# Joining the two matmuls that share their weights in the MLP block products

## The chip, the cores and the metric

The kernel runs on one core of one Trainium2 chip, in one launch. The metric is the device time of one execution in microseconds (us). Three timed runs of the kernel before gave 2880.28, 2886.01 and 2888.11 us; the median is 2886.01 us. One further execution was profiled; it took 2884.02 us.

The engines are called by their names here: TensorE (in the profile PE for its matmuls and PEld for its weight loads), VectorE (DVE), ScalarE (ACT), GpSimd (POOL) and SyncE (SP), which issues the transfers. PSUM is the memory that TensorE writes its products to, in banks of 128 partitions x 512 float32; SBUF is the memory that holds everything else on the core.

## The reference

One layer of an encoder over 512 tokens with a model width of 2048: a mixer (neighbourhood attention and a gated delta rule), then an MLP, then a last normalisation. The change touches only the MLP. In the reference it is:

```python
hn = _rmsnorm(h, norm_mlp_w)
h = h + jnp.square(jax.nn.relu(hn @ w_mlp_up)) @ w_mlp_down
return _rmsnorm(h, norm_final_w)
```

`w_mlp_up` is 2048 x 8192 and `w_mlp_down` 8192 x 2048, both float32, as is the result.

## The kernel before

**Layout.** Activations lie transposed: 128 features in the partitions, the 512 tokens along the free axis. A unit of weights is a tile of 128 partitions x 1024 columns: eight blocks of 128 x 128 for one group of 128 output features, j = 0 to 7.

**Two parts for each operand.** Float32 numbers are multiplied as two parts in the type fp32r: a high part (a cast by ScalarE, tiles `wh`) and a low part (what the cast left over, subtracted by VectorE, tiles `wl`). `split`, lines 93 to 96, makes both. A product takes three matmuls: high x high, high x low and low x high.

**Block products.** The MLP multiplies in 2 x 2 blocks by a scheme with seven block products where the plain way has eight. The weights of a *pair* of output groups are four units: A11, A12, A21, A22. The 512 tokens are halved too. So a product is one weight unit, or a sum of units, times a moving operand of 1024 x 256. Each moving operand (names 11, 21, 22 and T1 to T4) lies ready in eight tiles of 128 x 512: columns 0 to 255 (`lo_t`) hold the high part, columns 256 to 511 (`hi_t`) the low part (`fill`, lines 857 to 859). The products are called Q4, P1, P5, P6, P3, P7 and P2, and stand in this order (`ORDER`, line 919). `run_product` (928 to 959) makes the weight sums S1 to S4 on VectorE, splits the weights, and calls `product` (899 to 908), which issues three matmuls of 256 columns for each j: lines 904, 905 and 906. Lines 904 and 905 have the same weights, the high part, and the two halves of the moving tile; all three add into the same 256 columns of one bank. Some products go on adding in a bank in which an earlier product already stands (`BANK` and `FIRST`, lines 917 and 918): P6 and P7 onto P1, P3 onto P5. So an earlier product is taken out before the next one adds to its bank.

**The up half.** 32 pairs, u0 to u31. `up_evac` (969 to 997) takes each product out of its bank: Q4, P5, P1 and P6 are copied to SBUF by ScalarE (tiles tA and tB), and P7, P3 and P2 are added to these copies by VectorE, which reads the bank. Then VectorE takes the minimum (r1) or maximum (r0) with zero and multiplies by the token's norm factor, ScalarE squares, and `differences` (1001 to 1011) makes the moving operands of the down half with four VectorE instructions and writes them to DRAM (`hidD`).

**The down half.** Four blocks b of the inner dimension, eight pairs each (names d0_0 to d3_7), two pairs at a time (`down_group`, 1079 to 1112). The first group of each block also loads and splits the moving operands (`operand_fill`, 1072 to 1077: 56 splits of 256 columns). Each product is added to or subtracted from the residual tiles h0 and h1 by VectorE, which reads the bank. `store` (1116 to 1129) writes them back to DRAM; the last group of the last block (pairs d3_6 and d3_7, with its own order of products, `keep`) stays on the core and ends the kernel with the final norm (`finish`, 1144 to 1153), in which GpSimd takes every third multiplication (line 1148).

**What sets the order.** Each engine works its own instructions in the order in which they stand. A scheduler places them: casts and low halves stand some two products ahead of the product that uses them. Tile pools hold the buffers: three for `wh` and `wl`, four for the raw weight units, seven for the tiles `a` of A22, A21 and of sums (line 1033), six for `et`, seven PSUM banks (line 785). A tile is written again only when its last reader is done. SyncE issues the transfers, one after the other.

Of the kernel before, what the change touches and what calls it, by code (L numbers as in the profile page):

```python
# [49 lines left out]
def tile_hybrid_block(  # L50
# [733 lines left out]
    with ExitStack() as p1:  # L784
# [76 lines left out]
        with ExitStack() as p5:  # L861
# [37 lines left out]
            def product(ps, w, o, first=False):  # L899
                hi, lo = w  # L900
                for j in range(8):
                    t = XS[o, j]
                    c = slice(j * 128, (j + 1) * 128)
                    PE.matmul(ps, hi[:, c], t[:, lo_t], start=first and j == 0, stop=False, skip_group_check=True)  # L904
                    PE.matmul(ps, hi[:, c], t[:, hi_t], start=False, stop=False, skip_group_check=True)  # L905
                    PE.matmul(ps, lo[:, c], t[:, lo_t], start=False, stop=j == 7, skip_group_check=True)  # L906
                    if j % NPUMP == NPUMP - 1:
                        pump()
# [12 lines left out]
            def open_pair(nm, a11, a12):  # L921
                p = Pair()
                p.nm, p.ps, p.step = nm, {}, 0
                p.a11, p.a12 = a11, a12
                p.keep = False
                return p

            def run_product(p, q, sums):
# [27 lines left out]
                if bk not in p.ps:  # L956
                    p.ps[bk] = bank()[:, 0:256]
                product(p.ps[bk], w, ROLE[q], q in FIRST)
# [10 lines left out]
            def up_evac(i, p, q, et):  # L969
# [5 lines left out]
                tA, tB, r0, r1 = p.tA, p.tB, p.r0, p.r1  # L975
                if q == "Q4":
                    S_.copy(out=tA[:, 0], in_=ps)
                elif q == "P5":
                    S_.copy(out=tA[:, 1], in_=ps)
                elif q == "P1":  # L980
                    S_.copy(out=tB[:, 0], in_=ps)
                elif q == "P6":
                    S_.copy(out=tB[:, 1], in_=ps)  # L983
                elif q == "P7":
                    add(r1.rearrange("p (o t) -> p o t", o=2), ps[:, None, :].to_broadcast([128, 2, 256]), tA)
                    V.scalar_tensor_tensor(out=r1, in0=r1, scalar=0.0, in1=rB, op0=ALU.min, op1=ALU.mult)
                    S_.activation(out=r1, in_=r1, func=AF.Square)
                elif q == "P3":
                    add(r0[:, hi_t], ps, tB[:, 1])
                else:  # L990
                    add(r0[:, lo_t], ps, tB[:, 0])
# [29 lines left out]
            for i, p in enumerate(first):  # L1021
                for q in ("P1", "P2"):
                    w = heads[i, q] or wsplit(p.a12, f"{q}_u{i}")
                    p.ps[BANK[q]] = bank()[:, 0:256]
                    product(p.ps[BANK[q]], w, ROLE[q], True)
# [3 lines left out]
        with ExitStack() as p6:  # L1029
            sm = p6.enter_context(tc.tile_pool(name="sm", bufs=1, side="right", reuse_waits="tile"))  # L1030

            def a_tile(name):
                return sm.tile([128, 1024], F32, tag="a", name=name, bufs=7)

            def et(name):
                return sm.tile([128, 2, 256], F32, tag="et", name=name, bufs=6)

# [5 lines left out]
            def up_group(idx, order, ps=None):  # L1043
# [4 lines left out]
                if order[0] == "P1":  # L1048
                    for q in ("P1", "P2"):
                        for i, p in zip(idx, ps):  # L1050
                            up_evac(i, p, q, et)
                    order = order[2:]
                for n, q in enumerate(order):
                    for i, p in zip(idx, ps):
                        run_product(p, q, a_tile)
                        up_evac(i, p, q, et)
# [22 lines left out]
            def down_group(b, idx, order, done):  # L1079
                ps = []  # L1080
                for i in idx:
                    p = open_pair(f"d{b}_{i}", load_raw(wdn[2 * i, 2 * b], f"A11_d{b}_{i}"), load_raw(wdn[2 * i, 2 * b + 1], f"A12_d{b}_{i}"))
                    more(p, wdn[2 * i + 1, 2 * b + 1], wdn[2 * i + 1, 2 * b])
                    p.keep = order is not ORDER
                    ps.append(p)
# [5 lines left out]
                for q in order:  # L1091
                    if idx[0] == 0:
                        operand_fill(b, ROLE[q])
                    for i, p in zip(idx, ps):
                        t = run_product(p, q, a_tile)
                        h0, h1 = p.h0, p.h1
                        if q == "Q4":
# [187 lines left out]
```

## Time and profile before

| what | value |
|---|---|
| median of three runs | 2886.01 us (2880.28 to 2888.11) |
| profiled execution: its time, its span | 2884.02 us, 2881.9 us |
| TensorE matmul busy | 2811.9 us, 98% of the span |
| TensorE weight load busy | 2538.3 us, 88% |
| VectorE busy | 2065.1 us, 72% |
| ScalarE busy | 1167.0 us, 40% |
| GpSimd busy | 24.8 us, 1% |

The span is the time from the first to the last instruction of the profiled execution. "Busy" counts an instruction from its start to its end; matmuls overlap, so their rate is read from the distance between starts, not from their length. In the rows "L904" is line 904 of the kernel, "out<-in" names the tiles, "x768" how many instructions the row stands for.

### The profile page before, as it was taken

Reading aid. Unit: us, or ns where it says so; the run is one execution under the profiler, and the core shown is the slowest. Engines: PE = TensorE matmul, PEld = TensorE weight load, DVE = VectorE, ACT = ScalarE, POOL = GpSimd, SP = SyncE. Lnnn points to the kernel's source line nnn. Section 1 sums busy time; section 2 is a strip of 40 time slices with the busy share of each in tenths; the row PEclk is TensorE's granted clock in tenths of the full one; section 3 lists DMA queues with packets and bytes.
Section 4 is the critical chain, followed back from the end, with each engine's and each line's share of the span. In section 5 each row is a group of like instructions: output and inputs, shape, how many; then the busy total and the mean of one; then the engine's idle time right before and its main releaser. Section 6 shows DMA issues by size and latency. Waiting matters only on the chain.

```text
span 2881.9 us, 45456 instructions
## 1 busy us (share of the span) xinstructions
PE 2811.9 (98%) x17944; PEld 2538.3 (88%) x17944; DVE 2065.1 (72%) x3131; ACT 1167.0 (40%) x1869; POOL 24.8 (1%) x66
## 2 busy tenths in 40 slices
PE   8999999999999999999999999999998999999997
PEld 6778788888788888888888999999998999999997
DVE  6888769845564444444447888888888888898987
ACT  6444322223233333322335444444445354444543
POOL 0000010000000000000000000000000000000000
PEclk9999999999999999999999999999999999999998
DMA  7555663555642222533443445454447566565644
GB/s 228 191 187 189 196 198 120 183 173 182 181 140 93 87 93 84 199 133 125 142 145 137 153 151 156 143 162 147 149 146 228 180 222 201 170 226 174 221 133 146
DMA packets 217493, 469.32 MB, mean 163 GB/s; under 512 B 38976, under 2 KB 80000, under 8 KB 217280
## 3 DMA queue, kind: packets, MB, share of 16 engines
q1 hardware_dynamic: 216608, 464.33, 49.9%
q8 instruction: 140, 2.29, 0.3%
q0 software_dynamic: 672, 2.10, 0.3%
q14 instruction: 73, 0.60, 0.1%
HBM read 379.15 MB, written 87.20 MB: 162 GB/s over the span
## 4 chain that ended last, share of the span: by engine, by line
PE 78%; DMA 9%; DVE 9%; ACT 2%; issue 1%; SPq 0%; DVEq 0%; ACTq 0%
PE ps_b L906 12%; PE ps_b L904 12%; PE ps_b L905 12%; PE ps_mm L115 8%; PE ps_mm L117 8%; PE ps_mm L116 8%; PE ps_b L115 4%; PE ps_b L116 4%; PE ps_b L117 4%; DMA hr<-hidD 1%; DVE wl_S_d L95 1%; DVE wl_in L90 1%; DMA bB<-rowD 1%; DMA hTD<-h 1%; DMA Nd<-bB 1%
## 5 line engine op out<-in xcount | busy, mean ns | idle before, releaser
L115 PE MATMUL ps_mm<-xh,wh_in 128*128 128x512 f32 x1416 | 567.1, 400 | 3.1 <-ACT wh_in L89 3.1
L117 PE MATMUL ps_mm<-xh,wl_in 128*128 128x512 f32 x1416 | 559.9, 395 | 0.5 <-DVE wl_in L90 0.5
L116 PE MATMUL ps_mm<-xl,wh_in 128*128 128x512 f32 x1416 | 559.8, 395 | 0.0
L89 ACT CAST wh_in<-raw_in 128x1024 fp32r<-128x1024 f32 x177 | 186.0, 1051 | 412.9 <-PE ps_mm L116 328.5
L117 PEld LDWEIGHTS ps_mm<-xh,wl_in 128*128 128x128 f32 x1416 | 267.7, 189 | 60.4 <-DVE wl_in L90 1.0
L115 PEld LDWEIGHTS ps_mm<-xh,wh_in 128*128 128x128 f32 x1416 | 267.7, 189 | 58.6 <-ACT wh_in L89 3.5
L116 PEld LDWEIGHTS ps_mm<-xl,wh_in 128*128 128x128 f32 x1416 | 267.7, 189 | 55.0 <-issue 0.2
L90 DVE TENSOR_TENSOR wl_in<-raw_in,wh_in 128x1024 fp32r<-128x1024 f32 x177 | 216.2, 1222 | 118.7 <-ACT wh_in L89 110.2
L904 PE MATMUL ps_b<-XT_h,wh_S_d 128*128 128x256 f32 x768 | 220.8, 287 | 10.6 <-ACT wh_S_d L94 10.6
L906 PE MATMUL ps_b<-XT_h,wl_S_d 128*128 128x256 f32 x768 | 220.9, 288 | 3.2 <-DVE wl_S_d L95 3.1
L905 PE MATMUL ps_b<-XT_h,wh_S_d 128*128 128x256 f32 x768 | 219.8, 286 | 0.0
L906 PE MATMUL ps_b<-XT_x,wl_S_u 128*128 128x256 f32 x768 | 217.4, 283 | 0.8 <-DVE wl_S_u L95 0.8
L904 PE MATMUL ps_b<-XT_x,wh_S_u 128*128 128x256 f32 x768 | 217.4, 283 | 0.5 <-ACT tB_u L983 0.5
L905 PE MATMUL ps_b<-XT_x,wh_S_u 128*128 128x256 f32 x768 | 217.3, 283 | 0.0
L94 ACT CAST wh_S_u<-A_u 128x1024 fp32r<-128x1024 f32 x128 | 134.3, 1050 | 147.2 <-DVE A_u L911 81.2
L94 ACT CAST wh_S_d<-A_d 128x1024 fp32r<-128x1024 f32 x124 | 129.6, 1047 | 148.2 <-PE ps_b L905 129.0
L95 DVE TENSOR_TENSOR wl_S_u<-A_u,wh_S_u 128x1024 fp32r<-128x1024 f32 x128 | 156.0, 1222 | 39.4 <-ACT wh_S_u L94 39.4
L95 DVE TENSOR_TENSOR wl_S_d<-A_d,wh_S_d 128x1024 fp32r<-128x1024 f32 x124 | 151.2, 1222 | 23.9 <-ACT wh_S_d L94 22.2
L904 PEld LDWEIGHTS ps_b<-XT_h,wh_S_d 128*128 128x128 f32 x768 | 149.8, 195 | 12.5 <-ACT wh_S_d L94 12.5
L906 PEld LDWEIGHTS ps_b<-XT_h,wl_S_d 128*128 128x128 f32 x768 | 149.9, 195 | 5.0 <-DVE wl_S_d L95 5.0
L905 PEld LDWEIGHTS ps_b<-XT_h,wh_S_d 128*128 128x128 f32 x768 | 149.9, 195 | 0.0
L906 PEld LDWEIGHTS ps_b<-XT_x,wl_S_u 128*128 128x128 f32 x768 | 147.2, 192 | 1.0 <-DVE wl_S_u L95 1.0
(393 smaller groups left out, 7033.9 us busy)
## 6 DMA issues: line engine op xcount, KB each, us to landing
raw_in<-in_win SPq DMA_DIRECT2D x177, 512.0 KB
raw_A_u<-in_wup SPq DMA_DIRECT2D x64, 512.0 KB
A_u<-in_wup SPq DMA_DIRECT2D x64, 512.0 KB
A_d<-in_wdn SPq DMA_DIRECT2D x64, 512.0 KB
raw_A_d<-in_wdn SPq DMA_DIRECT2D x64, 512.0 KB
raw_wo<-in_wout SPq DMA_DIRECT2D x32, 512.0 KB
h<-hTD SPq DMA_DIRECT2D x64, 256.0 KB
hTD<-h SPq DMA_DIRECT2D x60, 256.0 KB
```

The costliest lines, as they stand in the source:

```text
L89: S_.copy(out=hi, in_=raw)
L90: V.tensor_tensor(out=lo, in0=raw, in1=hi.bitcast(F32), op=ALU.subtract)
L94: S_.copy(out=hi, in_=src)
L95: V.tensor_tensor(out=lo, in0=src, in1=hi.bitcast(F32), op=ALU.subtract)
L115: PE.matmul(ps, hi[:, w], rh, start=first and kk == 0, stop=False)
L116: PE.matmul(ps, hi[:, w], rl, start=False, stop=False)
L117: PE.matmul(ps, lo[:, w], rh, start=False, stop=last and kk == 7)
L904: PE.matmul(ps, hi[:, c], t[:, lo_t], start=first and j == 0, stop=False, skip_group_check=True)
L905: PE.matmul(ps, hi[:, c], t[:, hi_t], start=False, stop=False, skip_group_check=True)
L906: PE.matmul(ps, lo[:, c], t[:, lo_t], start=False, stop=j == 7, skip_group_check=True)
```

## The change

In `product` the two matmuls with the high weights become one of 512 columns: the high weights times the whole moving tile, into a whole bank of 512 columns. The low weights times the high half go, as before, into columns 0 to 255. For j = 7 the two stand the other way round. The product is then the sum of the bank's two halves. Every product's bank is copied whole by ScalarE into a tile `u` of SBUF (`spill`, pool tag "pr", two buffers), and GpSimd adds: where VectorE added from the bank before, and also the left to the right half. The seven `a` tiles become six. The last two pairs of the down half (`keep`) have the old form throughout. The weight sums, splits, ReLU steps, differences and fills stay on VectorE and ScalarE.

```diff
--- before.py
+++ after.py
@@ -896,11 +896,18 @@
                 lo = st.tile([128, 1024], F32R, tag="wl", name=f"wl_{name}", bufs=3)
                 return split(raw, hi, lo)
 
-            def product(ps, w, o, first=False):
+            def product(ps, w, o, first=False, whole=True):
                 hi, lo = w
                 for j in range(8):
                     t = XS[o, j]
                     c = slice(j * 128, (j + 1) * 128)
+                    if whole:
+                        mms = [(ps, hi, t), (ps[:, lo_t], lo, t[:, lo_t])]
+                        for n, (dst, a, b) in enumerate(mms if j < 7 else mms[::-1]):
+                            PE.matmul(dst, a[:, c], b, start=first and j + n == 0, stop=j == 7 and n == 1, skip_group_check=True)
+                        if j % NPUMP == NPUMP - 1:
+                            pump()
+                        continue
                     PE.matmul(ps, hi[:, c], t[:, lo_t], start=first and j == 0, stop=False, skip_group_check=True)
                     PE.matmul(ps, hi[:, c], t[:, hi_t], start=False, stop=False, skip_group_check=True)
                     PE.matmul(ps, lo[:, c], t[:, lo_t], start=False, stop=j == 7, skip_group_check=True)
@@ -923,6 +930,7 @@
                 p.nm, p.ps, p.step = nm, {}, 0
                 p.a11, p.a12 = a11, a12
                 p.keep = False
+                p.whole = True
                 return p
 
             def run_product(p, q, sums):
@@ -954,8 +962,8 @@
                     w = wsplit(p.s2, f"S4_{nm}")
                 bk = BANK[q]
                 if bk not in p.ps:
-                    p.ps[bk] = bank()[:, 0:256]
-                product(p.ps[bk], w, ROLE[q], q in FIRST)
+                    p.ps[bk] = bank() if p.whole else bank()[:, lo_t]
+                product(p.ps[bk], w, ROLE[q], q in FIRST, p.whole)
                 return p.ps[bk]
 
             def up_m(i):
@@ -966,29 +974,31 @@
                 m0, m1 = up_m(i)
                 return open_pair(f"u{i}", load_raw(wup[m0, 0], f"A11_u{i}"), load_raw(wup[m0, 1], f"A12_u{i}"))
 
-            def up_evac(i, p, q, et):
+            def gsum(out, x, y, op=ALU.add):
+                G.tensor_tensor(out=out, in0=x, in1=y, op=op)
+
+            def up_evac(i, p, q, et, spill):
                 ps = p.ps[BANK[q]]
                 if not hasattr(p, "tA"):
                     p.tA, p.tB = et(f"tA_u{i}"), et(f"tB_u{i}")
                     p.r0, p.r1 = ev(f"r0_u{i}"), ev(f"r1_u{i}")
                     p.left = 7
                 tA, tB, r0, r1 = p.tA, p.tB, p.r0, p.r1
+                u = spill(ps, f"u{q}_u{i}")
                 if q == "Q4":
-                    S_.copy(out=tA[:, 0], in_=ps)
+                    gsum(tA[:, 0], u[:, 0], u[:, 1])
                 elif q == "P5":
-                    S_.copy(out=tA[:, 1], in_=ps)
-                elif q == "P1":
-                    S_.copy(out=tB[:, 0], in_=ps)
-                elif q == "P6":
-                    S_.copy(out=tB[:, 1], in_=ps)
+                    gsum(tA[:, 1], u[:, 0], u[:, 1])
                 elif q == "P7":
-                    add(r1.rearrange("p (o t) -> p o t", o=2), ps[:, None, :].to_broadcast([128, 2, 256]), tA)
+                    gsum(u[:, 0], u[:, 0], u[:, 1])
+                    gsum(r1.rearrange("p (o t) -> p o t", o=2), u[:, 0:1, :].to_broadcast([128, 2, 256]), tA)
                     V.scalar_tensor_tensor(out=r1, in0=r1, scalar=0.0, in1=rB, op0=ALU.min, op1=ALU.mult)
                     S_.activation(out=r1, in_=r1, func=AF.Square)
-                elif q == "P3":
-                    add(r0[:, hi_t], ps, tB[:, 1])
                 else:
-                    add(r0[:, lo_t], ps, tB[:, 0])
+                    dst = r0[:, lo_t] if q in ("P1", "P2") else r0[:, hi_t]
+                    gsum(dst, dst if q in ("P2", "P3") else u[:, 1], u[:, 0])
+                    if q in ("P2", "P3"):
+                        gsum(dst, dst, u[:, 1])
                 p.left -= 1
                 if p.left:
                     return
@@ -1021,7 +1031,7 @@
             for i, p in enumerate(first):
                 for q in ("P1", "P2"):
                     w = heads[i, q] or wsplit(p.a12, f"{q}_u{i}")
-                    p.ps[BANK[q]] = bank()[:, 0:256]
+                    p.ps[BANK[q]] = bank()
                     product(p.ps[BANK[q]], w, ROLE[q], True)
             for o, j in early_fill[8:]:
                 fill(o, j, tr_src[o, j])
@@ -1030,10 +1040,15 @@
             sm = p6.enter_context(tc.tile_pool(name="sm", bufs=1, side="right", reuse_waits="tile"))
 
             def a_tile(name):
-                return sm.tile([128, 1024], F32, tag="a", name=name, bufs=7)
+                return sm.tile([128, 1024], F32, tag="a", name=name, bufs=6)
 
             def et(name):
                 return sm.tile([128, 2, 256], F32, tag="et", name=name, bufs=6)
+
+            def spill(ps, name):
+                u = sm.tile([128, 2, 256], F32, tag="pr", name=name, bufs=2)
+                S_.copy(out=u.rearrange("p a b -> p (a b)"), in_=ps)
+                return u
 
             def more(p, s22, s21):
                 p.a22, p.a21 = a_tile(f"A22_{p.nm}"), a_tile(f"A21_{p.nm}")
@@ -1048,12 +1063,12 @@
                 if order[0] == "P1":
                     for q in ("P1", "P2"):
                         for i, p in zip(idx, ps):
-                            up_evac(i, p, q, et)
+                            up_evac(i, p, q, et, spill)
                     order = order[2:]
                 for n, q in enumerate(order):
                     for i, p in zip(idx, ps):
                         run_product(p, q, a_tile)
-                        up_evac(i, p, q, et)
+                        up_evac(i, p, q, et, spill)
                     if n == 2:
                         while late:
                             late.pop(0)()
@@ -1082,6 +1097,7 @@
                     p = open_pair(f"d{b}_{i}", load_raw(wdn[2 * i, 2 * b], f"A11_d{b}_{i}"), load_raw(wdn[2 * i, 2 * b + 1], f"A12_d{b}_{i}"))
                     more(p, wdn[2 * i + 1, 2 * b + 1], wdn[2 * i + 1, 2 * b])
                     p.keep = order is not ORDER
+                    p.whole = not p.keep
                     ps.append(p)
                 for e in (1, 0):
                     for i, p in zip(idx, ps):
@@ -1094,7 +1110,17 @@
                     for i, p in zip(idx, ps):
                         t = run_product(p, q, a_tile)
                         h0, h1 = p.h0, p.h1
-                        if q == "Q4":
+                        if p.whole:
+                            u = spill(t, f"u{q}_{p.nm}")
+                            if q == "P7":
+                                gsum(u[:, 0], u[:, 0], u[:, 1])
+                                hv = h1.rearrange("p (o t) -> p o t", o=2)
+                                gsum(hv, hv, u[:, 0:1, :].to_broadcast([128, 2, 256]), ALU.subtract)
+                            else:
+                                dst = (h1 if q in ("Q4", "P5") else h0)[:, lo_t if q in ("Q4", "P1", "P2") else hi_t]
+                                for k in range(2):
+                                    gsum(dst, dst, u[:, k], ALU.subtract if q in ("Q4", "P5") else ALU.add)
+                        elif q == "Q4":
                             add(h1[:, lo_t], h1[:, lo_t], t, ALU.subtract)
                         elif q == "P5":
                             add(h1[:, hi_t], h1[:, hi_t], t, ALU.subtract)
```

On **ScalarE**, in up pair 10 from the copy of Q4 on, there stood (ps_b is a bank, wh_S2, wh_S4, wh_S3 are casts of the weights of P6, P3 and P7; tA and tB are the copies of banks):

```order
L977 COPY tA_u10_14553<-ps_b_14528 128x256
L996 ACTIVATE r0_u9_14320<-r0_u9_14320 128x512
L94 CAST wh_S2_u10_14629<-A22_u10_14520 128x1024
L981 COPY tB_u10_14554<-ps_b_14562 128x256
L94 CAST wh_S4_u10_14659<-A22_u10_14520 128x1024
L979 COPY tA_u10_14553<-ps_b_14593 128x256
L94 CAST wh_S3_u10_14689<-A21_u10_14521 128x1024
```

and now stand (uQ4, uP1, uP5, uP6 are the bank copies into the two "pr" tiles):

```order
L94 CAST wh_S1_u10_14187<-A22_u10_14130 128x1024
L1006 ACTIVATE r0_u9_13961<-r0_u9_13961 128x512
L1050 COPY uQ4_u10_14159<-ps_b_14138 128x512
L94 CAST wh_S2_u10_14221<-A22_u10_14130 128x1024
L1050 COPY uP1_u10_14183<-ps_b_14166 128x512
L94 CAST wh_S4_u10_14245<-A22_u10_14130 128x1024
L1050 COPY uP5_u10_14208<-ps_b_14191 128x512
L94 CAST wh_S3_u10_14270<-A21_u10_14131 128x1024
L1050 COPY uP6_u10_14241<-ps_b_14166 128x512
```

Each product now has a 512-wide copy, and it stands ahead of the cast of the weights that come three products later.

On **VectorE**, at the change from pair 9 to pair 10, there stood (r1_u9 and r0_u9 are pair 9's results, A22_u10 and A21_u10 weights or their sums, wl low parts):

```order
L95 TENSOR_TENSOR wl_A22_u10_14525<-A22_u10_14520,wh_A22_u10_14524 128x1024
L911 TENSOR_TENSOR A22_u10_14520<-A22_u10_14520,A21_u10_14521 128x1024
L911 TENSOR_TENSOR r1_u9_14321<-ps_b_14327,tA_u9_14318 128x512
L95 TENSOR_TENSOR wl_A11_u10_14559<-raw_A11_u10_14516,wh_A11_u10_14558 128x1024
L986 SCALAR_TENSOR_TENSOR r1_u9_14321<-r1_u9_14321,rB_79 128x512
L911 TENSOR_TENSOR A21_u10_14521<-A21_u10_14521,raw_A11_u10_14516 128x1024
L911 TENSOR_TENSOR r0_u9_14320<-ps_b_14293,tB_u9_14319 128x256
L95 TENSOR_TENSOR wl_S1_u10_14590<-A22_u10_14520,wh_S1_u10_14589 128x1024
```

and now stand:

```order
L95 TENSOR_TENSOR wl_A22_u10_14135<-A22_u10_14130,wh_A22_u10_14134 128x1024
L918 TENSOR_TENSOR A22_u10_14130<-A22_u10_14130,A21_u10_14131 128x1024
L918 TENSOR_TENSOR A21_u10_14131<-A21_u10_14131,raw_A11_u10_14126 128x1024
L995 SCALAR_TENSOR_TENSOR r1_u9_13962<-r1_u9_13962,rB_79 128x512
L95 TENSOR_TENSOR wl_A11_u10_14163<-raw_A11_u10_14126,wh_A11_u10_14162 128x1024
L1005 SCALAR_TENSOR_TENSOR r0_u9_13961<-r0_u9_13961,rB_79 128x512
L95 TENSOR_TENSOR wl_S1_u10_14188<-A22_u10_14130,wh_S1_u10_14187 128x1024
```

The two additions that read a bank (r1_u9 and r0_u9 from ps_b) are gone; the ReLU steps of r1_u9 and r0_u9 still stand ahead of the low parts of A11 and S1 of pair 10.

On **GpSimd**, which had nothing to do in the MLP before, now stand for pair 10 ("x2" are two such instructions in a row):

```order
L978 TENSOR_TENSOR tA_u10_14155<-uQ4_u10_14159 128x256
L978 TENSOR_TENSOR r0_u10_14157<-uP1_u10_14183 128x256
L978 TENSOR_TENSOR tA_u10_14155<-uP5_u10_14208 128x256
L978 TENSOR_TENSOR r0_u10_14157<-uP6_u10_14241 128x256
L978 TENSOR_TENSOR r0_u10_14157<-r0_u10_14157,uP3_u10_14265 128x256 x2
L978 TENSOR_TENSOR uP7_u10_14290<-uP7_u10_14290 128x256
L978 TENSOR_TENSOR r1_u10_14158<-uP7_u10_14290,tA_u10_14155 128x512
L978 TENSOR_TENSOR r0_u10_14157<-r0_u10_14157,uP2_u10_14316 128x256 x2
```

Ten instructions: nine additions of 256 columns and one of 512, and GpSimd, not VectorE, now hands r0 and r1 to the ReLU step.

## Rows read from the trace of the kernel before

**Rows 1.** The page's head and part 1: busy us, share of span, instructions.
```profile
span 2881.9 us, 45456 instructions
PE 2811.9 (98%) x17944; PEld 2538.3 (88%) x17944; DVE 2065.1 (72%) x3131; ACT 1167.0 (40%) x1869; POOL 24.8 (1%) x66
```

**Rows 2.** The page's part 4: chain that ended last, shares by engine.
```profile
PE 78%; DMA 9%; DVE 9%; ACT 2%; issue 1%; SPq 0%; DVEq 0%; ACTq 0%
```

**Rows 3.** Product matmuls of line 904: duration ns min/median/max, first and last start us.
```profile
L904 PE MATMUL ps_b<-X_x,wh_P_u x32: 279/282/365, 1530.6 to 1543.5; 128*128 128x256 f32 x32
...
L904 PE MATMUL ps_b<-XT_h,wh_A_d x256: 280/283/283, 2188.4 to 2824.7; 128*128 128x256 f32 x128
...
L904 PE MATMUL ps_b<-X_h,wh_S_d x256: 280/283/469, 2221.5 to 2861.0; 128*128 128x256 f32 x128
```

**Rows 4.** Up half, 200 us: busy us and instructions by engine, clock, DMA.
```profile
1680.00:1880.00 200.00, 200.00 (x1672) 200.00 (x1671) 169.59 (x200) 96.50 (x130) 0.00 (x0) 1.00 0.48 151
```

**Rows 5.** TensorE's waits in the down half: us in total, times, longest us.
```profile
PE ps_b L904 <- ACT wh_S_d L94: 11.7, 11, 2.4
PE ps_b L906 <- DVE wl_S_d L95: 3.1, 6, 0.8
PE ps_b L906 <- DVE wl_A_d L95: 0.4, 1, 0.4
```

**Rows 6.** TensorE's timeline in the up half: start us, duration us, instruction.
```profile
2000.10 0.28 PE L904 MATMUL ps_b<-X_x,wh_S_u 128*128 128x256 f32 x1
...
2003.94 0.28 PE L906 MATMUL ps_b<-XT_x,wl_S_u 128*128 128x256 f32 x1
```

**Rows 7.** TensorE's timeline where matmuls have 512 columns (ahead of the MLP).
```profile
1250.67 0.39 PE L115 MATMUL ps_b<-ybh,wh_pb 128*128 128x512 f32 x1
...
1252.30 0.40 PE L116 MATMUL ps_b<-ybl,wh_pb 128*128 128x512 f32 x1
```

**Rows 8.** ScalarE's groups by shape: busy us, mean ns, idle before.
```profile
L389 ACT COPY vt<-ps_ax 128x512 f32<-128x512 f32 x8 | 4.7, 586 | 10.9 <-PE ps_ax L137 10.9
```

**Rows 9.** VectorE's groups by shape in 400 us of the up half.
```profile
L95 DVE TENSOR_TENSOR wl_S_u<-A_u,wh_S_u 128x1024 fp32r<-128x1024 f32 x80 | 97.6, 1222 | 23.4 <-ACT wh_S_u L94 23.4
L911 DVE TENSOR_TENSOR A_u<-A_u,raw_A_u 128x1024 f32<-128x1024 f32 x60 | 73.3, 1221 | 0.7
...
L911 DVE TENSOR_TENSOR r_u<-ps_b,tB_u 128x256 f32<-128x256 f32 x40 | 16.9, 422 | 14.2 <-PE ps_b L906 14.2
L986 DVE SCALAR_TENSOR_TENSOR r_u<-r_u,rB 128x512 f32<-128x512 f32 x20 | 13.7, 685 | 0.0
...
L911 DVE TENSOR_TENSOR r_u<-ps_b,tA_u 128x512 f32<-128x512 f32 x20 | 13.7, 684 | 0.0
L1006 DVE SCALAR_TENSOR_TENSOR tA_u<-tA_u,r_u 128x256 f32<-128x256 f32 x20 | 8.5, 425 | 0.7
```

**Rows 10.** VectorE's timeline in the up half, three instructions back to back.
```profile
2005.70 1.21 DVE L95 TENSOR_TENSOR wl_A_u<-raw_A_u,wh_A_u 128x1024 fp32r<-128x1024 f32 x1
2006.84 0.68 DVE L986 SCALAR_TENSOR_TENSOR r_u<-r_u,rB 128x512 f32<-128x512 f32 x1
2007.44 1.22 DVE L911 TENSOR_TENSOR A_u<-A_u,raw_A_u 128x1024 f32<-128x1024 f32 x1
```

**Rows 11.** VectorE's timeline in the kernel's tail.
```profile
2857.69 2.74 DVE L1150 TENSOR_TENSOR Hf<-ps_b,Hf 128x256 f32<-128x256 f32 x8 [1.20 <-ACT rB L1166]
```

**Rows 12.** VectorE's groups by shape, 2300 to 2780 us: fills and bank additions.
```profile
L911 DVE TENSOR_TENSOR h<-ps_b,h 128x256 f32<-128x256 f32 x94 | 39.5, 420 | 15.4 <-PE ps_b L906 15.4
...
L95 DVE TENSOR_TENSOR XT_h<-hr3T,XT_h 128x256 fp32r<-128x256 f32 x32 | 12.6, 418 | 0.0
```

**Rows 13.** GpSimd's groups by shape.
```profile
L1148 POOL TENSOR_TENSOR Hf<-Hf,rB 128x256 f32<-128x256 f32 x8 | 5.6, 736 | 1752.6 <-ACT rB L1166 1752.6
```

**Rows 14.** GpSimd's timeline in the same stretch of the tail as rows 11.
```profile
2857.74 2.84 POOL L1148 TENSOR_TENSOR Hf<-Hf,rB 128x256 f32<-128x256 f32 x4 [1743.04 <-ACT rB L1166]
2860.53 0.75 POOL L1148 TENSOR_TENSOR h<-h,rB 128x256 f32<-128x256 f32 x1
```

## The prediction

> **What bounds the kernel now.** I read the page's head and busy times first, then the chain, then windows and waits of the MLP, then single instructions. The page has TensorE busy for 98% of the 2881.9 us span and VectorE for 72% [rows 1]. The chain that ended last is 78% TensorE, DMA and VectorE 9% each [rows 2]. The MLP products start at 1530.6 us, the up half gives way to the down half at 2188.4 us, and the last product matmuls start just after 2861.0 us [rows 3]: 46% of the span, the only part that the change touches. In the up half 200 us hold 1672 matmuls without a gap, so a pair of blocks (7 products x 24 matmuls = 168) takes 168 x 200/1672 = 20.10 us; VectorE is busy for 169.59 of the 200, GpSimd for nothing [rows 4]. In the down half TensorE waits 11.7 + 3.1 + 0.4 us, for casts of ScalarE and for VectorE's low halves [rows 5]. So TensorE is the bound and VectorE the next one, at 85 to 87%.
>
> **TensorE's part.** Starts of 256-column matmuls lie 0.120 us apart (32 steps from 2000.10 to 2003.94) [rows 6], those of 512 columns 0.233 us (7 steps from 1250.67 to 1252.30) [rows 7]. One step j of a product was 3 x 0.120 = 0.360 us and becomes 0.233 + 0.120 = 0.353. A 512 followed by a 256 is not in the trace. Bounds: 1.5 x 0.233 = 0.350 if columns alone count, 0.360 if nothing is saved. I take 0.353, the sum of the two rows. 434 products change (7 x 62 pairs; the last two pairs of the down half keep the old form), 8 steps each: 3472 x 0.007 = 24 us less, at most 35. A pair then needs 56 x 0.353 = 19.77 us of TensorE.
>
> **ScalarE's part.** Every product's bank is now copied by ScalarE, 512 wide. The 512-wide copy out of PSUM takes 0.586 us [rows 8]: 7 x 0.586 = 4.1 us a pair, in the up half in place of four narrow ones. ScalarE is busy 96.50 of 200 us there, 9.7 us a pair [rows 4]; with 4.1 more it is under 14 of 20. Hidden, cost nothing as engine time.
>
> **What VectorE sheds and keeps.** Per up pair it loses one 512-wide and two 256-wide additions that read PSUM, per down pair one and six. What it keeps reads two SBUF operands in each instruction: seven low halves and four weight sums of 1024 columns; in the up half also two 512-wide ReLU steps and four 256-wide differences [rows 9]. Back to back, a 1024 starts 1.14 us before its successor (2005.70 to 2006.84), a 512 0.60 (2006.84 to 2007.44) [rows 10], and a 256 0.33 (8 in 2.74, the last lasting 0.42) [rows 11]. Up pair: 11 x 1.14 + 2 x 0.60 + 4 x 0.33 = 15.1 us. Down pair: 12.5 us, and for each of the four blocks 56 fills of 256 columns [rows 12], 56 x 0.33 = 18.5 us; six statistics additions of 0.60 come once.
>
> **What GpSimd gets.** Per up pair nine additions of 256 columns and one of 512; per down pair 13 and one. Its addition-like instruction of 256 columns takes 0.736 us [rows 13]; four in 2.84 us start 0.70 apart [rows 14]. The 512-wide one isn't in the trace. Bounds: 0.74 (width costs nothing) and 1.47 (twice). VectorE's 512 against 256 is 685 to 422 ns [rows 9], and by that ratio it is 1.2, which I take. Up: 9 x 0.70 + 1.2 = 7.5 us. Down: 13 x 0.70 + 1.2 = 10.3 us. Both are far below 19.8, so GpSimd by itself is no bound.
>
> **The open cost: do GpSimd and VectorE run beside each other?** This decides the sign. The only place where both work at once is the tail: four GpSimd multiplications in 2.84 us beside eight VectorE ones in 2.74, neither stretched [rows 11, 14]. But there VectorE reads one operand from PSUM and one from SBUF; in the MLP after the change each VectorE instruction reads two from SBUF. So the row nearest in engine and size differs in what is in question. Let f be the share of GpSimd's time in which VectorE stands still, or the other way round. At f = 0 nothing is added. At f = 1 both take turns, and an up pair takes 15.1 + 7.5 = 22.6 us, a down pair 12.5 + 10.3 = 22.8 us. I take f = 1, as a choice: GpSimd needs 0.70 us for what VectorE does in 0.33, so it gets its two operands at half the rate, which looks like one path; and the penalty doesn't need f = 1: VectorE has to finish inside TensorE's time, and 15.1 + 7.5f passes the old 20.1 us at f = 0.67.
> The Trainium skill, page "SBUF — State Buffer", section "Who interferes with whom", speaks against this change: VectorE's second read path is GpSimd's only one, and a VectorE instruction with two SBUF inputs and a GpSimd instruction that reads SBUF shut each other out for a whole instruction. By that rule f is 1 and the sum the one below; without it, rival B. The trace agrees only in that the one-operand case runs free; no row shows two operands.
>
> Sum at f = 1, without idle. Up: 32 x (22.6 - 20.1) = +80 us. Down: 30 x 22.8 + 4 x 18.5 + 6 x 0.60 = 762 us. The same 30 pairs now take 2861.0 - 2188.4 = 673 less two pairs at 20.1, 633 us: +129 us. Together +209 us on the profiled execution's 2884.0 us: 3093; that execution is 2 us under the median of the runs, so 3095 us. TensorE's 24 us are not in it, as TensorE would then wait.
> Upper end: whole durations in place of start distances. VectorE up 11 x 1.222 + 2 x 0.685 + 4 x 0.425 = 16.5, GpSimd 9 x 0.736 + 1.47 = 8.1, together 24.6; down 13.4 + 13 x 0.736 + 1.47 = 24.5, a block's fills 56 x 0.418 = 23.4. That is +144 us up and 30 x 24.5 + 94 + 4 - 633 = +200 down: 3230 us. Lower end at f = 0.75: up 15.1 + 5.6 = 20.7 (+19 us); down 30 x (12.5 + 7.7) + 78 - 633 = +51: 2956 us.
>
> **How the delay gets to TensorE; the waits added.** A spill (the ScalarE copy into one of two "pr" tiles) waits until GpSimd has added the product two before it. Behind it in ScalarE's order stands the cast of the weights three products on; VectorE's low half waits for that cast, TensorE for both. On VectorE the ReLU step of r1 now waits for GpSimd's two additions of P7, and behind it stands the low half of A11 of the next pair. Alone: spill 0.6, additions 0.7 + 1.2, ReLU 0.6, low half 1.14 make 4.2 us after P7, and P1 needs it two products (5.6 us) later: hidden with 1.4 us to spare. Taking turns uses that up: each GpSimd instruction can stand behind a 1.14 us one. The seventh weight tile goes (6 in place of 7): SyncE's loads of A22 go out later, but TensorE's waits name no DMA [rows 5] and the up loads still go two pairs ahead. Cost between nothing and, in 12 down groups, the longest single wait in those rows, 12 x 2.4 = 29 us; I take nothing.
>
> **Rivals.**
> A (forecast), they take turns: 3095 us.
> B, on the other side: they run beside each other (f under about 0.55 in both halves). Place: every product's additions, hidden behind 2.8 us of TensorE. VectorE falls to 15.1 of 19.8 us, TensorE stays the bound and gains 24 us; of the 15 us that it waits in the down half up to all may go, since VectorE loses eight additions there. 2884 - 24 - (0 to 15) + 2 = 2847 to 2862; I take 2855. For it: the unstretched tail. Against it: there one operand came from PSUM.
> C, a draw: f near 0.6, where the shared time just equals TensorE's old time; 2875 to 2956 us. VectorE's 15% of idle time speaks for it, the down half's larger additions against.
> D, worse than turns: handing over leaves both idle, or a GpSimd instruction in the MLP costs much more than in the tail. Two additions per down product exceed TensorE's 2.83 us from 1.41 us each, twice the row. Over 3230 us.
>
> **Numbers.** A 0.68, B 0.21, C 0.06, D 0.05. Within 0.3% (about what a measurement of this kernel can tell from no change) means 2877 to 2895: 0.01 of B and 0.03 of C. Faster 0.20, same 0.04, slower 0.76. A's own range is 2956 to 3230. Leaving B out would leave 0.26 outside, so the range goes down to B's 2850; up to 3235.
>
> **What the changed profile would show.** Steps of 0.353 us in a product right or wrong at once. If A: VectorE's 1024-wide instructions or GpSimd's 256-wide ones far over 1.22 and 0.74 us, TensorE waiting in each pair for ScalarE's casts and VectorE's low halves, up pairs of 22 to 24 us. If B: durations as before, GpSimd busy for some 7.5 us of 19.8, TensorE without waits. Wrong would be a slow kernel with unstretched durations: then a wait on the "pr" tiles or a late load is the cause; or a fast kernel with both engines' instructions overlapping in time.

## The result and the profile after

The changed kernel takes 3094.43 us (median of four runs, 3093.36 to 3098.77) against 2883.66 us for the kernel before (four runs too): a ratio of 1.074, 95% interval 1.072 to 1.076. The forecast was 3095 us. The profiled execution has a span of 3092.7 us, 210.8 more than before.

The page's head, busy times and the chain by engine, which answer to [rows 1, 2]:

```profile
span 3092.7 us, 39929 instructions
PE 2863.3 (93%) x14472; PEld 2363.4 (76%) x14472; DVE 2234.9 (72%) x2825; ACT 1338.7 (43%) x2175; POOL 979.0 (32%) x806
PE 41%; DVE 20%; issue 19%; POOL 8%; DMA 7%; ACT 5%; SPq 0%; DVEq 0%; POOLq 0%; ACTq 0%
```

TensorE's share of the chain fell from 78% to 41%; VectorE, GpSimd and "issue" took its place. VectorE is busy for longer, though 306 instructions were taken from it. Starts of products of the down half (line 907); they answer to [rows 3]:

```profile
L907 PE MATMUL ps_b<-XT_h,wh_A_d x240: 387/396/796, 2306.4 to 2982.1; 128*128 128x512 f32 x120
```

The down half now begins at 2306.4 us, 118 later than the 2188.4 before. The other 93 us of the 211 were lost behind it. In the up half 400 us hold 1915 matmuls, 112 to a pair, so a pair takes 23.4 us where it took 20.1 [rows 4]:

```profile
1680.00:2080.00 400.00, 361.20 (x1915) 300.57 (x1914) 333.65 (x291) 200.76 (x273) 206.42 (x172) 0.97 0.41 129
```

VectorE's groups in the same 400 us (about 17 pairs), to be laid beside [rows 9], and GpSimd's, beside [rows 13]:

```profile
L95 DVE TENSOR_TENSOR wl_S_u<-A_u,wh_S_u 128x1024 fp32r<-128x1024 f32 x68 | 87.3, 1284 | 24.3 <-ACT wh_S_u L94 22.4
L918 DVE TENSOR_TENSOR A_u<-A_u,raw_A_u 128x1024 f32<-128x1024 f32 x52 | 87.2, 1677 | 1.2
L95 DVE TENSOR_TENSOR wl_A_u<-raw_A_u,wh_A_u 128x1024 fp32r<-128x1024 f32 x34 | 58.8, 1729 | 0.0
L95 DVE TENSOR_TENSOR wl_A_u<-A_u,wh_A_u 128x1024 fp32r<-128x1024 f32 x17 | 30.6, 1799 | 20.2 <-ACT wh_A_u L94 20.2
L918 DVE TENSOR_TENSOR A_u<-A_u,A_u 128x1024 f32<-128x1024 f32 x18 | 22.1, 1226 | 0.6
L995 DVE SCALAR_TENSOR_TENSOR r_u<-r_u,rB 128x512 f32<-128x512 f32 x17 | 20.5, 1208 | 20.0 <-POOL r_u L978 20.0
```

```profile
L978 POOL TENSOR_TENSOR r_u<-r_u,uP_u 128x256 f32<-128x256 f32 x68 | 55.4, 815 | 27.1 <-ACT uP_u L1050 24.4
L978 POOL TENSOR_TENSOR r_u<-uP_u 128x256 f32<-128x256 f32 x34 | 47.9, 1410 | 48.9 <-ACT uP_u L1050 46.6
L978 POOL TENSOR_TENSOR r_u<-uP_u,tA_u 128x512 f32<-128x512 f32 x18 | 38.7, 2150 | 1.4
L978 POOL TENSOR_TENSOR uP_u<-uP_u 128x256 f32<-128x256 f32 x18 | 31.1, 1730 | 21.7 <-ACT uP_u L1050 19.0 <-DMA raw_A_u<-in_wup 2.7
```

The same 1024-wide addition that took 1221 ns takes 1677, a low half of a raw unit 1729, the first ReLU step 1208 in place of 685; the groups of 256-wide GpSimd additions take 815 to 1730 where the tail's takes 736. One place shows both engines at it; first VectorE, then GpSimd:

```profile
1800.76 1.21 DVE L995 SCALAR_TENSOR_TENSOR r_u<-r_u,rB 128x512 f32<-128x512 f32 x1 [1.18 <-POOL r_u L978]
1801.89 1.74 DVE L95 TENSOR_TENSOR wl_A_u<-raw_A_u,wh_A_u 128x1024 fp32r<-128x1024 f32 x1
1803.55 0.68 DVE L1005 SCALAR_TENSOR_TENSOR r_u<-r_u,rB 128x512 f32<-128x512 f32 x1
```

```profile
1798.58 2.15 POOL L978 TENSOR_TENSOR r_u<-uP_u,tA_u 128x512 f32<-128x512 f32 x1
1800.68 1.86 POOL L978 TENSOR_TENSOR r_u<-r_u,uP_u 128x256 f32<-128x256 f32 x2
```

While GpSimd's two additions run (1800.68 to 1802.54) VectorE's ReLU step and low half are both about 0.5 us too long; the next ReLU step, with GpSimd done, has its usual 0.68. TensorE's main waits (us in total, times, longest) in the up half, then in the down half, the latter to be laid beside [rows 5]:

```profile
PE ps_b L907 <- DVE wl_A_u L95: 53.4, 30, 1.8
```

```profile
PE ps_b L907 <- DVE wl_S_d L95: 37.5, 48, 2.4
PE ps_b L907 <- DVE wl_A_d L95: 30.6, 39, 2.7
PE ps_b L907 <- DVE XT_h L95: 19.3, 1, 19.3
```

TensorE waits for VectorE's low halves, in 30 of the 32 up pairs for that of A11, the instruction that stands behind the ReLU step.

The 19.3 us are a single wait between the two halves, just ahead of 2306.4 us. The fills of the first down products need tiles that SyncE loads from `hidD`. The first of these loads, before and now:

```profile
2159.22 0.32 SPq L1075 DMA_DIRECT2D hr0T<-hidD  x1
2300.59 0.46 SPq L1090 DMA_DIRECT2D hr0T<-hidD  x1
```

Before, it went out 29 us ahead of the first down product. Now it stands in SyncE's order behind the last up pairs' writes to `hidD`, the last of which goes out at 2299.06 us. The prediction had no term for this.

### The profile page after: what moved, and what is told of

Read it like the earlier page. It is cut to its first block, busy times and chain, and to the rows that moved or that the text cites. A ratio compares the mean times of both kernels' runs of the same rounds, so it can differ in the third digit from the quotient of the medians.

```text
span 3092.7 us, 39929 instructions
## 1 busy us (share of the span) xinstructions
PE 2863.3 (93%) x14472; PEld 2363.4 (76%) x14472; DVE 2234.9 (72%) x2825; ACT 1338.7 (43%) x2175; POOL 979.0 (32%) x806
## 4 chain that ended last, share of the span: by engine, by line
PE 41%; DVE 20%; issue 19%; POOL 8%; DMA 7%; ACT 5%; SPq 0%; DVEq 0%; POOLq 0%; ACTq 0%
PE ps_b L907 12%; PE ps_mm L115 8%; PE ps_mm L117 8%; PE ps_mm L116 8%; POOL r_u L978 3%; DVE wl_S_d L95 3%; POOL h L978 3%; DVE A_u L918 2%; DVE wl_S_u L95 2%; DVE A_d L918 2%; DVE wl_A_d L95 2%; POOL uP_u L978 2%; DVE wl_A_u L95 1%; ACT wh_S_u L94 1%; DVE X_h L95 1%
## 5 line engine op out<-in xcount | busy, mean ns | idle before, releaser
L978 POOL TENSOR_TENSOR h<-h,uP_d 128x256 f32<-128x256 f32 (+1 forms) x330 | 460.1, 1404 | 122.9 <-ACT uP_d L1050 108.6
L90 DVE TENSOR_TENSOR wl_in<-raw_in,wh_in 128x1024 fp32r<-128x1024 f32 x177 | 216.2, 1222 | 120.7 <-ACT wh_in L89 111.9
L907 PE MATMUL ps_b<-XT_x,wh_S_u 128*128 128x512 f32 x768 | 276.9, 400 | 1.8 <-ACT wh_S_u L94 1.8
L907 PE MATMUL ps_b<-XT_h,wh_S_d 128*128 128x512 f32 x720 | 261.4, 406 | 7.8 <-ACT wh_S_d L94 7.8
L978 POOL TENSOR_TENSOR r_u<-uP_u 128x256 f32<-128x256 f32 x64 | 86.7, 1356 | 528.2 <-ACT uP_u L1050 524.0
L907 PE MATMUL ps_b<-XT_h,wl_S_d 128*128 128x256 f32 x720 | 195.3, 292 | 26.5 <-DVE wl_S_d L95 26.3
L95 DVE TENSOR_TENSOR wl_S_d<-A_d,wh_S_d 128x1024 fp32r<-128x1024 f32 x124 | 192.9, 1564 | 27.7 <-ACT wh_S_d L94 27.7
L907 PE MATMUL ps_b<-X_x,wh_A_u 128*128 128x512 f32 x480 | 191.1, 425 | 0.0
L1050 ACT COPY uP_d<-ps_b 128x512 f32<-128x512 f32 x180 | 105.2, 585 | 187.7 <-POOL h L978 102.1
L907 PE MATMUL ps_b<-X_x,wl_A_u 128*128 128x256 f32 x480 | 136.7, 306 | 50.6 <-DVE wl_A_u L95 50.6
L907 PE MATMUL ps_b<-X_h,wh_A_d 128*128 128x512 f32 x480 | 176.5, 406 | 2.4 <-ACT wh_A_d L94 2.4
```

Source lines behind the costliest of these rows:

```text
L90: V.tensor_tensor(out=lo, in0=raw, in1=hi.bitcast(F32), op=ALU.subtract)
L95: V.tensor_tensor(out=lo, in0=src, in1=hi.bitcast(F32), op=ALU.subtract)
L907: PE.matmul(dst, a[:, c], b, start=first and j + n == 0, stop=j == 7 and n == 1, skip_group_check=True)
L978: G.tensor_tensor(out=out, in0=x, in1=y, op=op)
L1050: S_.copy(out=u.rearrange("p a b -> p (a b)"), in_=ps)
```

## The experiments

**Side by side, alone.** A kernel of its own with trains of independent instructions (arguments shortened):

```
v_two : V.tensor_tensor(out=c, in0=a, in1=b)            # 128x1024, two SBUF tiles
v_bank: V.tensor_tensor(out=c, in0=ps, in1=a)           # 128x512, a bank and an SBUF tile
v_one : V.tensor_scalar(out=c, in0=a, ...)              # 128x1024, one SBUF tile
g_two : G.tensor_tensor(out=f, in0=d, in1=e)            # 128x256
g_one : G.tensor_copy(out=f, in_=d)    g_none: G.memset(f)
```

> A kernel by itself that computes nothing of the layer: trains of VectorE and GpSimd instructions on tiles that have nothing to do with each other, in stretches one after the other. VectorE: 1024-wide additions of two SBUF tiles, 512-wide additions of a bank and an SBUF tile, 1024-wide scalings of one tile; GpSimd: 256-wide additions, copies and fills. Theory 1 (turns, where VectorE takes two SBUF operands and GpSimd reads SBUF): 40 VectorE additions and 40 GpSimd ones last 40 x 1.14 + 40 x 0.70 = 74 us together; beside bank additions and beside fills each engine keeps its own time (28 us for 40 GpSimd additions, 46 us for 40 VectorE ones). Theory 2 (side by side): 46 us, the longer of the two, in every stretch.

VectorE's trains, then GpSimd's (start, length of the whole train):

```profile
6.64 27.34 DVE L40 TENSOR_TENSOR vc<-va,vb 128x1024 f32<-128x1024 f32 x24 [0.90 <-DMA vb<-in_x]
51.69 66.06 DVE L40 TENSOR_TENSOR vc<-va,vb 128x1024 f32<-128x1024 f32 x40 [17.71 <-ACT va L63]
118.80 43.14 DVE L43 TENSOR_TENSOR vc<-ps,va 128x512 f32<-128x512 f32 x72 [1.05 <-ACT va L63]
162.49 45.50 DVE L40 TENSOR_TENSOR vc<-va,vb 128x1024 f32<-128x1024 f32 x40 [0.55 <-ACT va L63]
208.53 53.23 DVE L40 TENSOR_TENSOR vc<-va,vb 128x1024 f32<-128x1024 f32 x40 [0.55 <-ACT va L63]
269.35 44.73 DVE L46 TENSOR_SCALAR vc<-va 128x1024 f32<-128x1024 f32 x40 [7.58 <-ACT va L63]
315.12 14.44 DVE L43 TENSOR_TENSOR vc<-ps,va 128x512 f32<-128x512 f32 x24 [1.05 <-ACT va L63]
330.09 14.54 DVE L46 TENSOR_SCALAR vc<-va 128x1024 f32<-128x1024 f32 x24 [0.53 <-ACT va L63]
```

```profile
34.86 16.36 POOL L49 TENSOR_TENSOR gc<-ga,gb 128x256 f32<-128x256 f32 x24 [33.07 <-ACT ga L64]
52.10 66.22 POOL L49 TENSOR_TENSOR gc<-ga,gb 128x256 f32<-128x256 f32 x40 [0.89 <-ACT ga L64]
119.21 27.34 POOL L49 TENSOR_TENSOR gc<-ga,gb 128x256 f32<-128x256 f32 x40 [0.89 <-ACT ga L64]
146.48 15.27 POOL L55 MEMSET gc<- 128x256 f32 x60
162.51 7.31 POOL L55 MEMSET gc<- 128x256 f32 x20 [0.77 <-ACT va L63]
208.87 60.01 POOL L52 COPY gc<-ga 128x256 f32<-128x256 f32 x60 [39.05 <-ACT ga L64]
269.77 44.89 POOL L49 TENSOR_TENSOR gc<-ga,gb 128x256 f32<-128x256 f32 x40 [0.89 <-ACT ga L64]
345.56 8.28 POOL L52 COPY gc<-ga 128x256 f32<-128x256 f32 x24 [30.91 <-ACT ga L64]
```

Alone a VectorE addition costs 27.34/24 = 1.14 us and a GpSimd one 16.36/24 = 0.68. Forty of each beside each other last 66.6 us (51.69 to 118.32), where the longer train alone has 45.5 and both after each other 72.8. They take turns, but save some 0.16 us at each pair of instructions. Beside bank additions 40 GpSimd additions last 27.34 us, 0.68 each as alone, and VectorE's bank additions 0.60 each (43.14/72), also as alone (14.44/24). Beside fills VectorE's additions keep their 1.14 us (45.50/40); 20 of the 80 fills ran beside them, in the first 7.3 us. Theory 1 holds in kind; its 74 us were 7 too many.

**Write only.** The changed kernel with each addition replaced by fills:

```diff
-            def gsum(out, x, y, op=ALU.add):
-                G.tensor_tensor(out=out, in0=x, in1=y, op=op)
+            def gsum(out, u, n=2):
+                for k in range(n):
+                    G.memset(u[:, k], 0.0)
+                G.memset(out, 0.0)
```

> The changed kernel with each GpSimd addition replaced by three fills (both halves of the copied bank and the result), which write but read nothing; the sums are left out. GpSimd has 3 x 0.31 us in place of each 0.70, 9.5 us an up pair, and everyone waits for it as before, longer if anything. Theory 1, with reading as what excludes: VectorE's instructions keep 1.22 us, 2860 to 2885 us. Theory 1, with any GpSimd work excluding: 15.1 + 9.5 = 24.6 us an up pair, over 3090 us. Theory 2 (the chain): as slow as the changed kernel or slower, 3050 to 3150 us.

It took 2855.38 us, ratio 0.9906 (0.9885 to 0.9927): 28 us less than before and 5 under the range of theory 1. GpSimd has no less to do: it is busy for 598 us more than in the kernel before (623.2 against 24.8), where the additions, by the prediction's sums, need 32 x 7.5 + 30 x 10.3 = 549. VectorE's low halves of sums there, in the up half (its additions have 1222 ns):

```profile
L95 DVE TENSOR_TENSOR wl_S_u<-A_u,wh_S_u 128x1024 fp32r<-128x1024 f32 x77 | 93.6, 1224 | 48.6 <-ACT wh_S_u L94 48.3
```

So it is GpSimd's reading that stops VectorE. One restriction: the fills of results don't read the copies, and the scheduler set many of them earlier, so the chain behind the ReLU step is not as long here as expected. The next experiment keeps it. The gain lies in the down half, which begins at 2196.3 us, 8 later than before.

**Thin additions.** All additions stay in place, 8 columns wide:

```diff
-                G.tensor_tensor(out=out, in0=x, in1=y, op=op)
+                if fill:
+                    G.memset(out, 0.0)
+                G.tensor_tensor(out=out[..., 0:8], in0=x[..., 0:8], in1=y[..., 0:8], op=op)
```

> The changed kernel with every GpSimd addition only 8 columns wide, and a write-only fill of the tile ahead of it where nothing else writes it (the sums are left out, all copies, waits, joined matmuls and tile pools stay). Theory 1: almost no time to share: TensorE's bound, 2845 to 2865 us. Theory 2: the chain is about 1.5 to 3 us shorter but stands: 2850 to 2930 us. Theory 3: over 3000 us.

2868.03 us, ratio 0.9948 (0.993 to 0.9966), 3 us over the range of theory 1 and inside that of theory 2, which the next experiment tests. All copies, whole banks, the joined matmuls and the smaller pool are in it, so none of them makes the loss: theory 3 falls. One wait of the changed kernel stays: TensorE waits 14.3 us for the first fills of the down half, where the changed kernel has 19.3.

```profile
PE ps_b L907 <- DVE XT_h L95: 14.5, 2, 14.3
```

GpSimd's rows show how an instruction that has almost nothing to do still lasts until the VectorE instruction beside it ends. Two groups, then one addition with VectorE's low half beside it:

```profile
L980 POOL TENSOR_TENSOR r_u<-uP_u 128x8 f32<-128x8 f32 x40 | 30.1, 752 | 4.6 <-ACT uP_u L1052 4.3
...
L980 POOL TENSOR_TENSOR r_u<-uP_u,tA_u 128x16 f32<-128x16 f32 x20 | 4.4, 219 | 1.6
```

```profile
1815.23 1.23 DVE L95 TENSOR_TENSOR wl_S_u<-A_u,wh_S_u 128x1024 fp32r<-128x1024 f32 x1 [1.11 <-ACT wh_S_u L94]
1815.76 0.75 POOL L980 TENSOR_TENSOR tA_u<-uP_u 128x8 f32<-128x8 f32 x1 [2.84 <-DMA hidD<-r_u]
```

The 8-wide addition ends at 1816.51 us, VectorE's low half at 1816.46. The 8-wide additions of the first group take 752 ns; the 16-wide ones, which run while VectorE stands and waits for them, take 219.

**Nobody waits.** As many additions, results left in the "pr" tile:

```diff
-                    gsum(tA[:, 0], u[:, 0], u[:, 1])
...
+                gsum(u[:, 0], u[:, 0], u[:, 1])
...
-                    V.scalar_tensor_tensor(out=r1, in0=r1, scalar=0.0, in1=rB, op0=ALU.min, op1=ALU.mult)
+                    V.scalar_tensor_tensor(out=r1, in0=rB, scalar=0.0, in1=rB, op0=ALU.min, op1=ALU.mult)
```

> The changed kernel with as many GpSimd additions of the same widths, but their results are left in the pr tile and used by nobody: the ReLU steps read another tile and the residual tiles go back as they came (the MLP's result is left out). Only the pr tiles still make anyone wait for GpSimd. Theory 1: the shared time is the same, 22.6 us an up pair and 22.8 a down pair plus fills: 3040 to 3095 us. Theory 2: with nobody behind the chain the loss goes: 2855 to 2890 us.

3041.66 us, ratio 1.0551 (1.0531 to 1.0571), inside the range of theory 1: 158 of the 211 us remain with nobody behind the additions but the "pr" tiles. Theory 2, that the chain makes the whole loss, falls. The down half starts at 2280.6 us, 26 earlier than in the changed kernel; the wait of 19.3 us ahead of it isn't there in this kernel:

```profile
L907 PE MATMUL ps_b<-XT_h,wh_A_d x240: 387/396/628, 2280.6 to 2938.6; 128*128 128x512 f32 x120
```

**GpSimd with the old matmuls.** The evacuation without the join, which needs about half as much of GpSimd, shown against the kernel before:

```diff
-                    add(r0[:, hi_t], ps, tB[:, 1])
+                    gsum(r0[:, hi_t], spill(ps, f"u{q}_u{i}"), tB[:, 1])
...
+                            u = spill(t, f"u{q}_{p.nm}")
...
+                                gsum(dst, dst, u, ALU.subtract if q in ("Q4", "P5") else ALU.add)
```

> The other part alone: the old three matmuls of 256 columns, but GpSimd adds what VectorE added, from 256-wide ScalarE copies in the two pr tiles (six tiles a). GpSimd has half the work: 2 x 0.70 + 1.2 = 2.6 us in an up pair, 6 x 0.70 + 1.2 = 5.4 in a down pair. Theory 1: up 15.1 + 2.6 = 17.7 us of 20.1, no loss; down 8 x (12.5 + 5.4) + 18.5 = 162 us of 161 a block, at the limit: 2880 to 2930 us. Theory 2: the chain stays, one addition shorter: half or more of the loss remains, 2980 to 3060 us. Theory 3: 2884 us.

2934.02 us, ratio 1.0178 (1.0158 to 1.0197), 4 us over the range of theory 1: a quarter of the loss from 45% of the GpSimd time (2.6 and 5.4 us a pair for 7.5 and 10.3). In the up half, where the sum left 2.4 us of room in a pair, some 21 us are lost too: the down half begins at 2209.9 us, not at 2188.4. The stretches fall on single instructions; that TensorE comes to wait by this, with room elsewhere in the pair, is inferred:

```profile
L95 DVE TENSOR_TENSOR wl_S_u<-A_u,wh_S_u 128x1024 fp32r<-128x1024 f32 x78 | 95.0, 1221 | 23.4 <-ACT wh_S_u L94 23.4
...
L95 DVE TENSOR_TENSOR wl_A_u<-raw_A_u,wh_A_u 128x1024 fp32r<-128x1024 f32 x39 | 68.5, 1755 | 0.0
```

The low halves of sums keep 1221 ns. Those of the raw units have a mean of 1755: of the two in a pair, one meets P7's addition (2.32 us at 1815.22), the other doesn't (1.22 at 1808.32).

**Halves added by VectorE.** The join without GpSimd, shown against the changed kernel (the seventh weight tile is back too):

```diff
-                u = spill(ps, f"u{q}_u{i}")
...
-                    gsum(tA[:, 0], u[:, 0], u[:, 1])
...
+                    S_.copy(out=dst, in_=lh)
+                    add(dst, rh, dst)
...
+                    add(dst, lh, tB[:, k])
+                    add(dst, rh, dst)
```

> The joined 512-column matmuls stay, GpSimd's additions go: ScalarE copies the left half of a bank (Q4, P1, P5, P6, P7 of the up half) and VectorE adds the right half from the bank; in the down half VectorE adds both halves from the bank. Theory 1 (VectorE and GpSimd take turns): without GpSimd VectorE has 18.7 us of an up pair's 19.8, and in the down half 8 x 17.7 + 18.5 = 160 us of a block's 158, so the loss is gone: 2865 to 2910 us. Theory 2 (the engines run side by side, and the loss is the longer chain bank - ScalarE copy - GpSimd - ReLU step, with VectorE's queue standing behind it): 2865 to 2910 us as well. Theory 3 (the joined matmuls, whole banks themselves cost): stays over 3000 us.

2972.86 us, ratio 1.031 (1.0289 to 1.0331): all three theories missed it, two by 63 us, the third by 27 on the other side. In the up half no instruction is stretched, but VectorE is at 90%:

```profile
1680.00:2080.00 400.00, 383.15 (x2098) 319.42 (x2097) 361.88 (x504) 187.68 (x263) 0.00 (x0) 1.00 0.44 142
```

2098 matmuls in 400 us make 21.4 us a pair. The sum had 18.7 us of VectorE; it is busy for 19.3 (361.88/400 x 21.4) and idle for 2.1, in waits for casts and banks. That VectorE's fixed order can't fill these gaps is inferred. The down half begins 34 us late, at 2222.2; the other 56 us are lost behind it, where TensorE waits 47.3 us for ScalarE's casts. With the join the best kernel gains 28 us (write only), and the seven more additions of a pair cost more than that on either engine.

**ReLU steps later.** The chain's part in the up half:

```diff
-                    V.scalar_tensor_tensor(out=r1, in0=r1, scalar=0.0, in1=rB, op0=ALU.min, op1=ALU.mult)
-                    S_.activation(out=r1, in_=r1, func=AF.Square)
...
+                for r, op in ((r1, ALU.min), (r0, ALU.max)):
+                    V.scalar_tensor_tensor(out=r, in0=r, scalar=0.0, in1=rB, op0=op, op1=ALU.mult)
+                    S_.activation(out=r, in_=r, func=AF.Square)
```

> The changed kernel with the two ReLU steps of an up pair issued later, together with the differences, so that on VectorE the low half of the next pair's A11 stands ahead of them; all GpSimd additions stay. It sizes the chain's part in the up half, where a pair now takes 23.4 us. Theory 1 (turns): the shared time of about 21 to 22.6 us a pair stays and only VectorE's wait of 1.2 us for GpSimd goes: 3050 to 3080 us. Theory 2 (the chain alone): the up half returns to under 20 us a pair, 2960 to 2990 us.

3098.46 us, ratio 1.0749 (1.0723 to 1.0775): no gain, outside both ranges. TensorE's waits in the up half are now 33.7 us for low halves of sums and 30.4 for ScalarE's copies, in place of 53.4 for A11's low half. ScalarE's timeline shows that the wait moved by one place:

```profile
1804.65 0.63 ACT L1011 ACTIVATE r_u<-r_u 128x512 f32<-128x512 f32 x1 [0.69 <-DVE r_u L1010]
1805.19 0.56 ACT L1049 COPY uQ_u<-ps_b 128x512 f32<-128x512 f32 x1
1807.80 1.05 ACT L94 CAST wh_S_u<-A_u 128x1024 fp32r<-128x1024 f32 x1 [2.05 <-DVE A_u L918]
```

The squares wait for VectorE's ReLU steps (the second is shown), and Q4's copy and the next cast stand behind them. The up half's clock was 1.00 in this run against 0.97 in the changed kernel, at 23.5 against 23.4 us a pair (112 x 400/1909): the clock is no part of the up half's loss.

## Why the prediction was right

**TensorE's step.** Right. In the down half of the write-only kernel TensorE hardly stops, and 360 us hold 2038 matmuls, 0.353 us for two, as taken from two rows:

```profile
2400.00:2760.00 360.00, 359.63 (x2038) 311.35 (x2037) 275.75 (x313) 228.42 (x367) 140.28 (x529) 1.00 0.45 142
```

With GpSimd's reading gone or all but gone the kernel takes 2855 or 2868 us, where rival B had 2847 to 2862.

**ScalarE.** Right: a copy takes 585 ns, and ScalarE is busy for half of the time.

**Taking turns.** Right in kind: instructions are stretched on both sides, and none of VectorE's where GpSimd only writes or VectorE reads a bank. The rule of the Trainium skill, page "SBUF — State Buffer", section "Who interferes with whom", agrees in each case that was run: two SBUF inputs against a reading GpSimd instruction collide, while VectorE keeps its time with a bank as one of the two operands, or beside a fill. It has the loser blocked for the whole instruction; the 66.6 us in place of 72.8 show that a part of each instruction (0.16 us of the two) still overlaps.

**The sum.** The total was met within 1 us, and that was luck: its terms were not. Up half +80 foreseen, +118 measured; down half +129 foreseen, +93 measured. Two things were mis-sized. The share f (of GpSimd's time in which VectorE stands still) was not 1: in the trains it is (66.6 - 45.5)/27.3 = 0.77, and an up pair's VectorE instructions were stretched by 3.7 us (the groups' mean lengths add up to 20.2 us a pair, unstretched 16.5) for GpSimd's 7.5, a share of 0.49. At that share the prediction's formula has no loss in the up half: 15.1 + 3.7 = 18.8 us of 20.1. And the sum was made "without idle", which was wrong by about as much: VectorE is idle for 66 of 400 us, 3.9 a pair, more than the 3.1 before. At f = 0.77 and without idle, the prediction's own formula gives some 2970 us (up +25, down 30 x (12.5 + 7.9) + 78 - 633 = +57). The rest up to 3094, by subtraction, is time in which the engines wait for each other in their fixed orders. 19.3 us of it, inside the up half's +118, are the one wait for the first fills of the down half. Sharing doesn't make that wait: the thin kernel, which has next to nothing to share, has 14.3 us of it. The kernel in which nobody waits for the sums sizes 53 us of this time, that wait among them. For the other part no single wait was found, and the attempt to remove one only moved it. That stays open.

**The waits added.** Right in place: the ReLU step with A11's low half behind it is where TensorE waits 53.4 us in the up half. Alone, this chain was to take 4.2 us of the 5.6 that P1 leaves it. In the pair shown above it takes 7.56 us, from the start of P7's copy to the end of the low half (1803.63):

```profile
1796.07 0.59 ACT L1050 COPY uP_u<-ps_b 128x512 f32<-128x512 f32 x1 [1.25 <-PE ps_b L907]
1796.73 1.76 POOL L978 TENSOR_TENSOR uP_u<-uP_u 128x256 f32<-128x256 f32 x1 [1.17 <-ACT uP_u L1050]
```

GpSimd's two additions last 4.0 us (1796.73 to 1800.73) where 1.9 were counted, and TensorE waits 1.8. In the down half ScalarE's copies wait for GpSimd, 102 us between 2400 and 2960 us. The smaller pool costs nothing that can be seen (thin additions).

**Rivals.** B was excluded by the measurement, and the write-only kernel shows what it would have been. D, a hand-over that leaves both idle, is there in part: it is the idle time above, though the total stayed under its 3230 us.

## What to carry to other kernels

Before work goes to an idle GpSimd, count VectorE's instructions with two SBUF operands: both engines then have to fit into one engine's time, less about a tenth. A join on the busiest engine is worth only what the next engines can take on, and VectorE, in its fixed order, was in effect full at 90%: seven short additions a pair, on either engine, cost more than TensorE gained. Look at the seams between stages as well: a change inside a stage can move the loads of the next one behind its last writes. Check the terms of a sum against the stages; a total can be met by two errors.

## What the runs showed of the hardware

A VectorE instruction with a single SBUF operand can collide too. The 1024-wide scaling takes 14.54/24 = 0.61 us alone, half the addition's time, and 44.73/40 = 1.12 beside GpSimd's additions, which take 1.12 in place of 0.68. A GpSimd copy with one operand suffers more: 8.28/24 = 0.35 us alone; beside VectorE's additions the two go one for one, and 40 of each last 53.23 us, 1.33 each (the last 20 of the 60 copies ran when VectorE was done). In all three pairings two instructions that take turns last about 0.16 us less than the two alone: 1.14 + 0.68 against 1.66, 1.14 + 0.35 against 1.33, 0.61 + 0.68 against 1.12.

A fill doesn't hold VectorE up, but it comes slower itself: 7.31/20 = 0.37 us beside VectorE's additions of two SBUF tiles, 15.27/60 = 0.25 beside its bank additions. Why isn't shown.

In the profile the time that a GpSimd instruction stands still is inside its length, not in the idle time before it: an 8-wide addition with 752 ns, where 219 is enough for 16 columns, is the sign.
